# Feed-forward blocks of 256 and 290 token columns instead of 272 and 272

## The chip, the cores and the metric

The kernel runs on one core of one Trainium2 chip. The metric is device time of the program in microseconds (us), as the median of several runs. Beside the timed runs there is one execution recorded by the hardware profiler; all rows quoted below come from it.

The engines carry the profile's names: PE is the matmul engine (TensorE), PEld its weight loads, DVE the vector engine, ACT the scalar engine, POOL GpSimd, SP the engine that issues most transfers.

## The reference, cut to what matters

One decoder layer on 544 tokens: 512 of a prompt and 32 that are being decoded (8 sequences of 4). The layer is feed-forward block, mixer (a Mamba-2 group beside a sparse-attention group), feed-forward block, with a post-normalisation after each.

```python
def swiglu(x, w_gate, w_up, w_down):
    return (jax.nn.silu(x @ w_gate) * (x @ w_up)) @ w_down
...
h = layer_norm(ALPHA * x + 0.5 * swiglu(x, ffn1_w_gate, ffn1_w_up, ffn1_w_down), ln1_g, ln1_b)
mixed, state = mix_fn(h, lw, *mix_args)
h = layer_norm(ALPHA * h + mixed, ln2_g, ln2_b)
h = layer_norm(ALPHA * h + 0.5 * swiglu(h, ffn2_w_gate, ffn2_w_up, ffn2_w_down), ln3_g, ln3_b)
```

The model width is 1024, the feed-forward width 2816. All is computed to float32 accuracy.

## The kernel before

**Layout.** Tokens lie along the free dimension, channels on the 128 partitions. The 544 tokens stand as two halves of `HT` = 272 columns: `HP` = 256 prompt tokens and `HS` = 16 decoded ones each. The activations of a stage are eight tiles `XH[d]` and eight `XL[d]` (d = 0 to 7, the width in pieces of 128), each of two halves of 274 columns; columns 272 and 273 of half 0 hold, after a normalisation, its gain and bias, so that one matmul also yields the two sums per output channel that `fold` needs. Columns 272 and 273 of half 1 are never used.

**Matmuls.** Float32 accuracy is had by splitting each operand into a high part, rounded to the fast format float32r, and the rest: `XH` + `XL` for activations, `w_hi` + `w_lo` for weights. `gemm` (L256 to L265) makes three matmuls for each piece of 128 of the contraction: `w_hi` with the high part (L263), `w_hi` with the low part (L264), `w_lo` with the high part (L265). Each is preceded by a weight load of 128 columns. So one `gemm` over the model width is 8 x 3 = 24 matmuls into one PSUM tile.

**Feed-forward (`ffn`, L367).** Called twice. First 22 x 2 weight tiles (gate and up): for each weight tile one `gemm` per half h = 0, 1, then, on ACT and DVE, the Silu, the product and the split into `hH[:, f, h]` and `hL[:, f, h]`. In the second feed-forward block half 0 is multiplied with 274 columns. Then the eight output tiles of the down projection: 22 pieces x 3 matmuls for each half, in three weight tiles; `residual` adds the input on DVE, `Norm.tile` updates sums of the normalisation. For the last output tile (d = 7) half 0 is finished before half 1 begins, so that its tail can start.

**Order.** The program is written as loops, and a scheduler that simulates times places each instruction on its engine's queue; an engine runs its queue strictly in that order. Weights come by SP's queue through two raw buffers; ACT makes `w_hi` (L170), DVE or POOL `w_lo` (L171), three buffers each. The input x comes in four transfers (half 0 in two pieces of four tiles, then half 1), and ACT (L191) and DVE (L192) split each tile as it comes. The gate and up products use six PSUM tiles in turn.

Of the kernel before, what the change touches and what calls it, by code (L numbers as in the profile page):

```python
# [33 lines left out]

HP, HS = 256, 16
HT = HP + HS
D, KD = 1024, 8
DFF, KF = 2816, 22
ALPHA = 2.0 ** 0.25
# [136 lines left out]
def step_kernel(ctx, tc, I, O, stop=99):  # L176
    nc = tc.nc
    MUL, ADD, SUB, MAX = OP.mult, OP.add, OP.subtract, OP.max
# [4 lines left out]
    def f32(t):  # L183
        return t.bitcast(F32)
# [17 lines left out]
    eps1 = keep.tile([128, 1], F32, name="eps1")  # L202
    eps4 = keep.tile([128, 1], F32, name="eps4")
    XH, XL = [None] * KD, [None] * KD

    def new_x(d):
# [29 lines left out]
    with tc.tile_pool(name="xload", bufs=1) as xp:  # L236

        nc.vector.memset(eps1, LN_EPS)
        nc.scalar.activation(eps4, eps1, AF.Silu)
        W.load()  # L240
        for d in range(KD):
            new_x(d)
        for h in range(2):
            for a in range(2):
                xr = xp.tile([128, 4, HT], F32, name=f"xr{h}{a}")
                nc.sync.dma_start(xr, I["x"][h, :, 4 * a:4 * a + 4])
                if h == 0 and a == 1:
                    W.load()
                for d in range(4 * a, 4 * a + 4):
                    split(XH[d][:, h, :HT], XL[d][:, h, :HT], xr[:, d % 4])  # L250
        nc.gpsimd.dma_start(par, I["par"])
        cst(ident, "ident", nc.gpsimd)
        nc.vector.memset(ones, 1.0)
        nc.vector.memset(eps4, 4.0 * LN_EPS)

    def gemm(ps, wt, rhs, nk, k0=0, start=True, stop=True, m=128):  # L256

        hi, lo = wt
        rh, rl = rhs
# [18 lines left out]
    class Norm:  # L278
# [48 lines left out]

        def stats(self, pool, psum, halves=(0, 1), tag="st"):
            if 0 in halves:
                self.rstd = keep.tile([128, 2, HT], F32, name=f"rstd{self.n}", tag="rstd")  # L330
                self.nmr = keep.tile([128, 2, HT], F32, name=f"nmr{self.n}", tag="nmr")
# [18 lines left out]
        def fold(self, ps, h, cw, out, pool):  # L350

            m = cw.shape[0]
            if h == 0:
                nc.vector.tensor_copy(cw, ps[:m, HT:HT + 2])
            t = pool.tile([128, HT], F32, name="fold_t", bufs=2)
            nc.vector.tensor_tensor(t[:m], ps[:m, :HT], self.rstd[:m, h], op=MUL)
            nc.vector.scalar_tensor_tensor(out, self.nmr[:m, h], cw[:, 0:1], t[:m], op0=MUL, op1=ADD)

        def value(self, d, out, pool, mul):

# [6 lines left out]
    def ffn(pre, post, last):  # L367

        with tc.tile_pool(name="ffn", bufs=1) as fp, tc.tile_pool(name="ffn_ps", bufs=1, space=PS) as pp:
            hH = fp.tile([128, KF, 2, HT], F32R, name="hH")  # L370
            hL = fp.tile([128, KF, 2, HT], F32R, name="hL")
            with tc.tile_pool(name="ffn_g", bufs=1) as gp:
                for f in range(KF):
                    sg = {}
                    for which in range(2):
                        wt = W.get()
                        cw = gp.tile([128, 2], F32, name="cw", bufs=4)
                        for h in range(2):
                            ps = pp.tile([128, 512], F32, name="mm", bufs=6)
                            rh, rl, n = xcols(h, pre is not None)  # L380
                            gemm(ps[:, :n], wt, (rh, rl), KD)
                            if f == 0 and which == 0 and h == 0 and pre is not None:
                                pre.stats(gp, pp)
                            if pre is None:
                                src = ps[:, :HT]
                            else:
                                src = gp.tile([128, HT], F32, name="fold_o", bufs=2)
                                pre.fold(ps, h, cw, src, gp)
                            if which == 0:
                                sg[h] = gp.tile([128, HT], F32, name="sg", bufs=3)  # L390
                                if pre is None:
                                    nc.scalar.activation(sg[h], src, AF.Silu)
                                else:
                                    nc.scalar.activation(sg[h], src, AF.Silu, bias=cw[:, 1:2])
                            else:
                                hf = gp.tile([128, HT], F32, name="hf", bufs=2)
                                if pre is None:
                                    nc.vector.tensor_tensor(hf, src, sg[h], op=MUL)
                                else:
                                    nc.vector.scalar_tensor_tensor(hf, src, cw[:, 1:2], sg[h], op0=ADD, op1=MUL)  # L400
                                split(hH[:, f, h], hL[:, f, h], hf)
            with tc.tile_pool(name="ffn_d", bufs=1) as dp:
                nrm = Norm(dp, *post, eps4, to_x=not last)

                tab = dp.tile([128, 1], F32, name="tab")
                nc.scalar.activation(tab, f32(hH)[:, KF - 1, 1, 0:1], AF.Sqrt, scale=0.0, bias=eps1)
                for d in range(KD):
                    t = dp.tile([128, 2, HT], F32, name="res", bufs=2)
                    if pre is None:
# [6 lines left out]
                    def down(i, h):  # L416
                        gemm(ps[h][:, :HT], wts[i], (lambda k: hH[:, k, h], lambda k: hL[:, k, h]),
                             min(8, KF - 8 * i), 8 * i, start=i == 0, stop=i == 2)

                    def residual(h):  # L420
                        nc.vector.scalar_tensor_tensor(t[:, h], t[:, h], 2.0 * ALPHA, ps[h][:, :HT],
                                                       op0=MUL, op1=ADD)

                    if d < KD - 1:
                        for i in range(3):
                            for h in range(2):
                                down(i, h)
                        for h in range(2):
                            residual(h)
                        if d == 0:  # L430
                            nrm.mean0(t, dp, pp)
                        nrm.tile(d, t, dp)
                    else:
                        for h in range(2):
                            for i in range(3):
                                down(i, h)
                            residual(h)
# [1058 lines left out]
```

## Time and profile before

| what | value |
|---|---|
| runs | 1319.51, 1320.40, 1321.38 us; median 1320.4 |
| profiled execution | 1316.73 us, of which the span from first to last instruction is 1315.0 |
| mean granted clock of PE | 0.975 of full speed |
| PE busy | 1250.2 us (95%) |
| DVE, ACT, POOL busy | 778.3, 479.1, 355.0 us |
| gate and up of the first feed-forward block | about 6 to 276.5 us |
| its down projection | 276.5 to 410 us |
| mixer | 411 to 886 us |
| gate and up of the second block | 886 to 1158 us |
| its down projection and the end | 1158 to 1315 us |

A busy time of PE counts the time in which any matmul is on its way; since matmuls overlap (each lasts some 0.29 us, and the next starts well before it ends), the time that one costs in a row of many is the distance from its start to the next start. This text calls it the pitch.

### The profile page before, as it was taken

The page shows a single profiled execution, that of the slowest core. Times are in us where ns is not written, and L with a number is a line of the kernel's source. Part 1 is how long each engine was busy: PE and PEld are TensorE (multiplying, and loading weights), DVE is VectorE, ACT ScalarE, POOL GpSimd, SP SyncE. Part 2 cuts the span into 40 slices and gives each one's busy share as a digit, 9 for nine tenths or more (in the row PEclk, how much of TensorE's full clock was granted, in tenths as well). Part 3 has the DMA queues.
Part 4 walks back from the last instruction along what each step waited for, and adds up shares of the span by engine and source line. Part 5 has one row for each costly group of instructions (what it writes and reads, how often), then busy time and mean ns, then how long its engine had stood idle before and what let it go on. Part 6 is the DMA issues. An engine that isn't in the chain of part 4 may idle for free.

```text
span 1315.0 us, 24300 instructions
## 1 busy us (share of the span) xinstructions
PE 1250.2 (95%) x9768; PEld 1178.3 (90%) x9768; DVE 778.3 (59%) x1510; ACT 479.1 (36%) x900; POOL 355.0 (27%) x289
## 2 busy tenths in 40 slices
PE   8999999999999888999999999779999999999994
PEld 7999999999999788888887676779999999999993
DVE  4333333334336888766798685997666666644446
ACT  4322223232224445454554332434333333342213
POOL 0000000001333653453555542770000000035543
PEclk9999999999999997999999998989999999999997
DMA  5222232222324324532232651222222232323211
GB/s 204 81 89 88 82 96 81 90 80 89 89 89 146 128 75 147 143 128 85 38 98 39 200 207 63 65 64 81 81 91 87 81 96 81 90 80 89 89 57 68
DMA packets 63888, 126.74 MB, mean 96 GB/s; under 512 B 16168, under 2 KB 35312, under 8 KB 63776
## 3 DMA queue, kind: packets, MB, share of 16 engines
q1 hardware_dynamic: 61040, 116.52, 29.3%
q0 software_dynamic: 1584, 4.48, 1.0%
q10 hardware_dynamic: 1152, 4.19, 0.8%
q8 instruction: 77, 1.26, 0.4%
q14 instruction: 35, 0.29, 0.1%
HBM read 114.80 MB, written 9.36 MB: 94 GB/s over the span
## 4 chain that ended last, share of the span: by engine, by line
PE 52%; DVE 7%; issue 1%; ACT 1%; DMA 1%; POOL 1%; ACTq 0%; POOLq 0%; DVEq 0%
PE mm L265 12%; PE mm L264 12%; PE mm L263 12%; PE pv L915 3%; PE pj L263 2%; PE pj L264 2%; PE pj L265 2%; PE tp L925 1%; PE sc L884 1%; PE sc L886 1%; DMA win<-in_vwin 1%; DVE XL L311 1%; DVE XL L326 1%; PE tp L1266 1%; PE sg L975 0%
## 5 line engine op out<-in xcount | busy, mean ns | idle before, releaser
L263 PE MATMUL mm<-XH,w_hi 128*128 128x272 f32 (+1 forms) x1408 | 409.1, 291 | 11.8 <-ACT XH L191 6.3
L265 PE MATMUL mm<-XH,w_lo 128*128 128x272 f32 (+1 forms) x1408 | 409.4, 291 | 0.0
L264 PE MATMUL mm<-XL,w_hi 128*128 128x272 f32 (+1 forms) x1408 | 408.4, 290 | 0.3 <-DVE XL L192 0.3
L171 DVE TENSOR_TENSOR w_lo<-w_raw,w_hi 128x1024 fp32r<-128x1024 f32 x149 | 183.6, 1232 | 205.1 <-ACT w_hi L170 203.4
L170 ACT ACTIVATE w_hi<-w_raw 128x1024 fp32r<-128x1024 f32 (+1 forms) x173 | 179.2, 1036 | 284.5 <-PE mm L264 231.9
L263 PEld LDWEIGHTS mm<-XH,w_hi 128*128 128x128 f32 x1408 | 268.1, 191 | 12.4 <-ACT XH L191 6.5
L264 PEld LDWEIGHTS mm<-XL,w_hi 128*128 128x128 f32 x1408 | 268.6, 191 | 0.7 <-DVE XL L192 0.6
L265 PEld LDWEIGHTS mm<-XH,w_lo 128*128 128x128 f32 x1408 | 267.4, 190 | 0.1
L265 PE MATMUL mm<-hH,w_lo 128*128 128x272 f32 x704 | 203.9, 290 | 0.0
L264 PE MATMUL mm<-hL,w_hi 128*128 128x272 f32 x704 | 203.4, 289 | 0.0
L263 PE MATMUL mm<-hH,w_hi 128*128 128x272 f32 x704 | 203.0, 288 | 0.0
L272 POOL TENSOR_TENSOR res<-XH,XL 128x544 f32<-128x544 f32 x24 | 35.0, 1468 | 588.9 <-DVE hL L192 550.0
L264 PEld LDWEIGHTS mm<-hL,w_hi 128*128 128x128 f32 x704 | 132.6, 188 | 0.2
L263 PEld LDWEIGHTS mm<-hH,w_hi 128*128 128x128 f32 x704 | 132.5, 188 | 0.1
L265 PEld LDWEIGHTS mm<-hH,w_lo 128*128 128x128 f32 x704 | 132.3, 188 | 0.2
L263 PE MATMUL pj<-XH,w_hi 128*128 128x272 f32 (+3 forms) x336 | 99.9, 297 | 7.0 <-DVE pj_u L640 5.8
L265 PE MATMUL pj<-XH,w_lo 128*128 128x272 f32 (+3 forms) x336 | 98.8, 294 | 0.0
L264 PE MATMUL pj<-XL,w_hi 128*128 128x272 f32 (+3 forms) x336 | 98.2, 292 | 0.0
L191 ACT ACTIVATE hH<-hf 128x272 fp32r<-128x272 f32 x88 | 37.5, 426 | 144.7 <-DVE hf L400 98.0
L263 PEld LDWEIGHTS pj<-XH,w_hi 128*128 128x128 f32 (+1 forms) x336 | 62.4, 186 | 11.2 <-issue 7.3
L321 POOL TENSOR_TENSOR accS<-res,accS 128x544 f32<-128x544 f32 x18 | 35.7, 1982 | 121.5 <-DVE res L307 121.5
L171 POOL TENSOR_TENSOR w_lo<-w_raw,w_hi 128x1024 fp32r<-128x1024 f32 (+1 forms) x24 | 56.8, 2365 | 38.4 <-ACT w_hi L170 38.4
(423 smaller groups left out, 2146.8 us busy)
## 6 DMA issues: line engine op xcount, KB each, us to landing
w_raw<-in_wg SPq DMA_DIRECT2D x44, 512.0 KB, 3.5
w_raw<-in_wu SPq DMA_DIRECT2D x44, 512.0 KB, 3.5
w_raw<-in_wd SPq DMA_DIRECT2D x32, 512.0 KB, 3.5
w_raw<-in_win SPq DMA_DIRECT2D x20, 512.0 KB, 3.6
pg<-in_cmp SPq DMA_DIRECT2D x64, 128.0 KB, 2.4
w_raw<-in_wd SPq DMA_DIRECT2D x16, 384.0 KB, 3.1
w_raw<-in_w SPq DMA_DIRECT2D x8, 512.0 KB, 3.7
pg<-in_kslc SPq DMA_DIRECT2D x64, 64.0 KB, 1.9
```

What stands on the lines that cost most here:

```text
L170: nc.scalar.activation(hi[:, :nk, :m], raw[:, :nk, :m], AF.Copy)
L171: (eng or nc.vector).tensor_tensor(lo[:, :nk, :m], raw[:, :nk, :m], hi.bitcast(F32)[:, :nk, :m], op=OP.subtract)
L191: nc.scalar.activation(hi, src, AF.Copy)
L263: nc.tensor.matmul(ps, hi[:, k, :m], rh(k0 + k), start=b, stop=False)
L264: nc.tensor.matmul(ps, hi[:, k, :m], rl(k0 + k), start=False, stop=False)
L265: nc.tensor.matmul(ps, lo[:, k, :m], rh(k0 + k), start=False, stop=e)
L272: nc.gpsimd.tensor_tensor(out, a, b, op=ADD)
L311: nc.vector.scalar_tensor_tensor(XL[d][:, h, :HT], s[:, h], self.g[:, d:d + 1], f32(XH[d])[:, h, :HT], op0=MUL, op1=SUB)
L321: eng.tensor_tensor(acc[:, h], v[:, h], acc[:, h], op=ADD)
L326: nc.vector.tensor_tensor(XL[d][o], col[:, d:d + 1], f32(XH[d])[o], op=SUB)
L884: nc.tensor.matmul(s, q, S.K[:, br, h // 4, 0, :w], start=True, stop=False)
L915: nc.tensor.matmul(pv[hh * 64:hh * 64 + 64, hp % 2], v, t[:, hh], start=start, stop=stop)
```

## The change

The 2 x 274 columns of an activation tile are now taken as one flat row of 548, of which columns 0 to 545 are multiplied, in two blocks: columns 0 to 255 (the first 256 prompt tokens) and columns 256 to 545 (16 decoded tokens, the two extra columns, the whole second half): 256 and 290 columns. `hH` and `hL` get rows of 548 columns. For each weight tile of gate and up the block of 290 stands first. `fold`, the Silu, the product and the split work on blocks. In the down projection of d = 0 to 6 the blocks replace the halves, and `residual` is three DVE instructions instead of two; d = 7 keeps halves of 272. New small memsets on POOL clear the two extra columns where nothing else writes them; two constants share one tile.

```diff
+WT = HT + 2
+BLK = (slice(0, HP), slice(HP, HT + WT))
...
+                    if h == 0:
+                        for t in (XH[d], XL[d]):
+                            nc.gpsimd.memset(f32(t)[:, 0, HT:], 0.0)
                     split(XH[d][:, h, :HT], XL[d][:, h, :HT], xr[:, d % 4])
...
+    def flat(t):
+        return t.rearrange("p a b -> p (a b)")
+
+    def xblk(c):
+        return (lambda k: flat(XH[k])[:, c]), (lambda k: flat(XL[k])[:, c])
...
-            hH = fp.tile([128, KF, 2, HT], F32R, name="hH")
-            hL = fp.tile([128, KF, 2, HT], F32R, name="hL")
+            hH = fp.tile([128, KF, 2 * WT], F32R, name="hH")
+            hL = fp.tile([128, KF, 2 * WT], F32R, name="hL")
...
-                        for h in range(2):
-                            ps = pp.tile([128, 512], F32, name="mm", bufs=6)
-                            rh, rl, n = xcols(h, pre is not None)
-                            gemm(ps[:, :n], wt, (rh, rl), KD)
-                            if f == 0 and which == 0 and h == 0 and pre is not None:
+                        for i in (1, 0):
+                            c = BLK[i]
+                            n = c.stop - c.start
+                            ps = pp.tile([128, 512], F32, name="mm", bufs=6)[:, :n]
+                            gemm(ps, wt, xblk(c), KD)
+                            if f == 0 and which == 0 and i == 1 and pre is not None:
                                 pre.stats(gp, pp)
...
                         for i in range(3):
-                            for h in range(2):
-                                down(i, h)
-                        for h in range(2):
-                            residual(h)
+                            for p, c in zip(ps, BLK):
+                                down(i, p, c)
+                        residual(t[:, 0, :HP], ps[0][:, :HP])
+                        residual(t[:, 0, HP:], ps[1][:, :HS])
+                        residual(t[:, 1], ps[1][:, HS + 2:HS + 2 + HT])
```

PE's queue at the start of the program, before: the last matmuls of the first `gemm` (PSUM tile mm_154, half 0 of all eight tiles), and then the first matmul that reads half 1 (into mm_181).

```order
L265 MATMUL mm_154<-XH6_85,w_lo_150 128x272
L263 MATMUL mm_154<-XH7_87,w_hi_149 128x272
L264 MATMUL mm_154<-XL7_88,w_hi_149 128x272
L265 MATMUL mm_154<-XH7_87,w_lo_150 128x272
L263 MATMUL mm_181<-XH0_73,w_hi_149 128x272
```

PE's queue at the same place now: mm_169 is the block of 290, mm_196 the block of 256 of the first weight tile.

```order
L270 MATMUL mm_169<-XH0_72,w_hi_164 128x290
L270 MATMUL mm_196<-XH0_72,w_hi_164 128x256
L271 MATMUL mm_196<-XL0_73,w_hi_164 128x256
L272 MATMUL mm_196<-XH0_72,w_lo_165 128x256
L270 MATMUL mm_196<-XH1_74,w_hi_164 128x256
```

A matmul that reads both halves of tile 0 is now PE's very first instruction; the 24 matmuls that read half 0 alone stood ahead of any such before.

DVE's queue early in the mixer, before, where `cp_lo` belongs to the compression of the prompt's keys and `QS` to the queries:

```order
L666 TENSOR_TENSOR pj_f_5363<-pj_f_5363,pj_sw_5364 128x544
L751 TENSOR_TENSOR cp_lo_5289<-cp_kc_5285,KcH_4332 64x32
L733 COPY cp_t_5445<-mm_5384 128x2
L751 TENSOR_TENSOR cp_lo_5295<-cp_kc_5285,KcH_4332 64x32
L734 TENSOR_TENSOR peb_4306<-cp_t_5445,mm_5384 128x1
L702 SCALAR_TENSOR_TENSOR QS_4320<-pj_f_5363,QS_4320 64x2x256 x2
```

And now:

```order
L687 TENSOR_TENSOR pj_f_5387<-pj_f_5387,pj_sw_5388 128x544
L723 SCALAR_TENSOR_TENSOR QS_4342<-pj_f_5387,QS_4342 64x2x256
L754 COPY cp_t_5469<-mm_5408 128x2
L723 SCALAR_TENSOR_TENSOR QS_4342<-pj_f_5387,QS_4342 64x2x256
L755 TENSOR_TENSOR peb_4328<-cp_t_5469,mm_5408 128x1
L175 TENSOR_TENSOR w_lo_5866<-w_raw_5863,w_hi_5865 128x1024
```

The scheduler moved the queries ahead of the compressed keys; further down that queue, for some 150 rows, attention steps and compression steps of the mixer are interleaved in another order, though no line of the mixer was edited.

## Rows read from the trace of the kernel before

**Rows 1.** Busy time of each engine in three stretches.
```profile
core 0: us, PE busy (x) PEld busy (x) DVE busy (x) ACT busy (x) POOL busy (x), PEclk, DMA share, GB/s
40.00:400.00 360.00, 360.00 (x2846) 359.84 (x2845) 129.51 (x187) 103.83 (x174) 33.48 (x20) 1.00 0.28 87
900.00:1157.00 257.00, 257.00 (x2027) 257.00 (x2026) 171.46 (x346) 89.40 (x133) 0.00 (x0) 1.00 0.28 88
500.00:520.00 20.00, 15.24 (x75) 14.95 (x76) 17.88 (x31) 10.55 (x24) 4.53 (x3) 0.57 0.62 174
```

**Rows 2.** Line L264: count, duration, first and last start; gate/up, then down, first block.
```profile
L264 PE MATMUL mm<-XL,w_hi x675: 286/289/294, 19.9 to 276.3; 128*128 128x272 f32 x169
...
L264 PE MATMUL mm<-hL,w_hi x284: 283/288/297, 297.9 to 404.8; 128*128 128x272 f32 x142
```

**Rows 3.** Timeline of PE, second block: start, duration; first matmuls of three successive gemms.
```profile
1017.98 0.28 PE L263 MATMUL mm<-XH,w_hi 128*128 128x274 f32 x1
...
1021.02 0.29 PE L263 MATMUL mm<-XH,w_hi 128*128 128x272 f32 x1
...
1024.07 0.28 PE L263 MATMUL mm<-XH,w_hi 128*128 128x274 f32 x1
```

**Rows 4.** Timeline of PE in the mixer: first and last of three runs of 256-column matmuls.
```profile
518.95 0.28 PE L263 MATMUL mm<-cs_H,w_hi 128*128 128x256 f32 x1
...
522.58 0.28 PE L265 MATMUL mm<-cs_H,w_lo 128*128 128x256 f32 x1
...
532.96 0.29 PE L264 MATMUL mm<-cs_L,w_hi 128*128 128x256 f32 x1
...
534.16 0.28 PE L265 MATMUL mm<-cs_H,w_lo 128*128 128x256 f32 x1
...
606.97 0.28 PE L263 MATMUL mm<-cs_H,w_hi 128*128 128x256 f32 x1
...
610.16 0.28 PE L263 MATMUL mm<-cs_H,w_hi 128*128 128x256 f32 x1
```

**Rows 5.** Timeline of PE in the mixer: one matmul of 512 columns and the next.
```profile
666.59 0.39 PE L884 MATMUL sc<-K,QS 128*128 128x512 f32 x1
666.82 0.23 PE L885 MATMUL sc<-mk_d,idb 128*128 128x128 bf16 x1
```

**Rows 6.** Timeline of PE in the mixer: matmuls of 66 columns at a lower clock, first and last of 27.
```profile
505.50 0.40 PE L263 MATMUL mm<-cH,w_hi 128*128 128x66 f32 x1
...
511.05 0.40 PE L265 MATMUL mm<-cH,w_lo 128*128 128x66 f32 x1
```

**Rows 7.** Timeline of PE at the start of the program.
```profile
6.25 0.59 PE L263 MATMUL mm<-XH,w_hi 128*128 128x272 f32 x1 [6.25 <-ACT XH L191]
...
8.21 0.43 PE L265 MATMUL mm<-XH,w_lo 128*128 128x272 f32 x1
...
10.02 0.41 PE L264 MATMUL mm<-XL,w_hi 128*128 128x272 f32 x1
10.24 0.31 PE L265 MATMUL mm<-XH,w_lo 128*128 128x272 f32 x1
10.39 0.29 PE L263 MATMUL mm<-XH,w_hi 128*128 128x272 f32 x1
...
11.40 0.29 PE L265 MATMUL mm<-XH,w_lo 128*128 128x272 f32 x1
11.69 0.52 PE L263 MATMUL mm<-XH,w_hi 128*128 128x272 f32 x2
```

**Rows 8.** Timeline of ACT: the splits of half 1, tiles 0 to 3, then 4 to 7.
```profile
11.21 1.40 ACT L191 ACTIVATE XH<-xr 128x272 fp32r<-128x272 f32 x4 [0.54 <-DMA xr<-in_x]
...
12.78 1.39 ACT L191 ACTIVATE XH<-xr 128x272 fp32r<-128x272 f32 x4
```

**Rows 9.** Start of the second block: PE, then DVE, then the busy time of a stretch.
```profile
885.74 0.57 PE L263 MATMUL mm<-XH,w_hi 128*128 128x274 f32 x1 [5.59 <-DVE res L607]
...
890.67 0.41 PE L263 MATMUL mm<-XH,w_hi 128*128 128x272 f32 x1
...
889.97 0.49 DVE L311 SCALAR_TENSOR_TENSOR XL<-res,par,XH 128x272 fp32r<-128x272 f32 x1
...
885.70:890.60 4.90, 4.86 (x21) 4.89 (x22) 4.76 (x9) 1.69 (x4) 0.74 (x1) 0.50 0.42 149
```

More of the change, by code (lines that the diff above doesn't have):

```diff
@@ L201, in step_kernel @@
     ones = keep.tile([128, 128], F32, name="ones")
-    eps1 = keep.tile([128, 1], F32, name="eps1")
-    eps4 = keep.tile([128, 1], F32, name="eps4")
+    eps = keep.tile([128, 2], F32, name="eps")
+    eps1, eps4 = eps[:, 0:1], eps[:, 1:2]
     XH, XL = [None] * KD, [None] * KD
@@ L329, in stats @@
             if 0 in halves:
-                self.rstd = keep.tile([128, 2, HT], F32, name=f"rstd{self.n}", tag="rstd")
-                self.nmr = keep.tile([128, 2, HT], F32, name=f"nmr{self.n}", tag="nmr")
+                self.rstd_w = keep.tile([128, 2, WT], F32, name=f"rstd{self.n}", tag="rstd")
+                self.nmr_w = keep.tile([128, 2, WT], F32, name=f"nmr{self.n}", tag="nmr")
+                self.rstd, self.nmr = (t[:, :, :HT] for t in (self.rstd_w, self.nmr_w))
+                if self.to_x:
+                    for t in (self.rstd_w, self.nmr_w):
+                        nc.gpsimd.memset(t[:, 0, HT:], 0.0)
             for h in halves:
@@ L348, in stats, with fold @@
                 nc.vector.scalar_tensor_tensor(self.nmr[:, h], mq[:, 0], -1.0, self.rstd[:, h], op0=MUL, op1=MUL)
[L350 to L357, printed above, removed]
+        def fold(self, ps, c, cw, out, pool):
+            n = c.stop - c.start
+            if c.start:
+                nc.vector.tensor_copy(cw, ps[:, HS:HS + 2])
+            t = pool.tile([128, BLK[1].stop - HP], F32, name="fold_t", bufs=2)
+            nc.vector.tensor_tensor(t[:, :n], ps, flat(self.rstd_w)[:, c], op=MUL)
+            nc.vector.scalar_tensor_tensor(out, flat(self.nmr_w)[:, c], cw[:, 0:1], t[:, :n], op0=MUL, op1=ADD)
         def value(self, d, out, pool, mul):
@@ L369, in ffn @@
         with tc.tile_pool(name="ffn", bufs=1) as fp, tc.tile_pool(name="ffn_ps", bufs=1, space=PS) as pp:
-            hH = fp.tile([128, KF, 2, HT], F32R, name="hH")
-            hL = fp.tile([128, KF, 2, HT], F32R, name="hL")
+            hH = fp.tile([128, KF, 2 * WT], F32R, name="hH")
+            hL = fp.tile([128, KF, 2 * WT], F32R, name="hL")
             with tc.tile_pool(name="ffn_g", bufs=1) as gp:
+                wide = BLK[1].stop - HP
                 for f in range(KF):
@@ L377, in ffn @@
                         cw = gp.tile([128, 2], F32, name="cw", bufs=4)
-                        for h in range(2):
-                            ps = pp.tile([128, 512], F32, name="mm", bufs=6)
-                            rh, rl, n = xcols(h, pre is not None)
-                            gemm(ps[:, :n], wt, (rh, rl), KD)
-                            if f == 0 and which == 0 and h == 0 and pre is not None:
+                        for i in (1, 0):
+                            c = BLK[i]
+                            n = c.stop - c.start
+                            ps = pp.tile([128, 512], F32, name="mm", bufs=6)[:, :n]
+                            gemm(ps, wt, xblk(c), KD)
+                            if f == 0 and which == 0 and i == 1 and pre is not None:
@@ L383, in ffn @@
                                 pre.stats(gp, pp)
                             if pre is None:
-                                src = ps[:, :HT]
+                                src = ps
                             else:
-                                src = gp.tile([128, HT], F32, name="fold_o", bufs=2)
-                                pre.fold(ps, h, cw, src, gp)
+                                src = gp.tile([128, wide], F32, name="fold_o", bufs=2)[:, :n]
+                                pre.fold(ps, c, cw, src, gp)
@@ L389, in ffn @@
                             if which == 0:
-                                sg[h] = gp.tile([128, HT], F32, name="sg", bufs=3)
+                                sg[i] = gp.tile([128, wide], F32, name="sg", bufs=3)[:, :n]
                                 if pre is None:
-                                    nc.scalar.activation(sg[h], src, AF.Silu)
+                                    nc.scalar.activation(sg[i], src, AF.Silu)
                                 else:
-                                    nc.scalar.activation(sg[h], src, AF.Silu, bias=cw[:, 1:2])
+                                    nc.scalar.activation(sg[i], src, AF.Silu, bias=cw[:, 1:2])
@@ L395, in ffn @@
                             else:
-                                hf = gp.tile([128, HT], F32, name="hf", bufs=2)
+                                hf = gp.tile([128, wide], F32, name="hf", bufs=2)[:, :n]
                                 if pre is None:
-                                    nc.vector.tensor_tensor(hf, src, sg[h], op=MUL)
+                                    nc.vector.tensor_tensor(hf, src, sg[i], op=MUL)
                                 else:
-                                    nc.vector.scalar_tensor_tensor(hf, src, cw[:, 1:2], sg[h], op0=ADD, op1=MUL)
@@ L401, in ffn @@
-                                split(hH[:, f, h], hL[:, f, h], hf)
+                                    nc.vector.scalar_tensor_tensor(hf, src, cw[:, 1:2], sg[i], op0=ADD, op1=MUL)
+                                split(hH[:, f, c], hL[:, f, c], hf)
             with tc.tile_pool(name="ffn_d", bufs=1) as dp:
@@ L405, in ffn @@
                 tab = dp.tile([128, 1], F32, name="tab")
-                nc.scalar.activation(tab, f32(hH)[:, KF - 1, 1, 0:1], AF.Sqrt, scale=0.0, bias=eps1)
+                nc.scalar.activation(tab, f32(hH)[:, KF - 1, 0:1], AF.Sqrt, scale=0.0, bias=eps1)
                 for d in range(KD):
@@ L414, in ffn, with down, residual @@
                     wts = [W.get() for _ in range(3)]
-                    def down(i, h):
-                        gemm(ps[h][:, :HT], wts[i], (lambda k: hH[:, k, h], lambda k: hL[:, k, h]),
+                    def down(i, p, c):
+                        gemm(p[:, :c.stop - c.start], wts[i], (lambda k: hH[:, k, c], lambda k: hL[:, k, c]),
                              min(8, KF - 8 * i), 8 * i, start=i == 0, stop=i == 2)
-                    def residual(h):
-                        nc.vector.scalar_tensor_tensor(t[:, h], t[:, h], 2.0 * ALPHA, ps[h][:, :HT],
-                                                       op0=MUL, op1=ADD)
+                    def residual(o, p):
+                        nc.vector.scalar_tensor_tensor(o, o, 2.0 * ALPHA, p, op0=MUL, op1=ADD)
                     if d < KD - 1:
                         for i in range(3):
-                            for h in range(2):
-                                down(i, h)
-                        for h in range(2):
-                            residual(h)
+                            for p, c in zip(ps, BLK):
[3 more added lines that the diff above has]
+                        residual(t[:, 1], ps[1][:, HS + 2:HS + 2 + HT])
                         if d == 0:
@@ L435, in ffn @@
                             for i in range(3):
-                                down(i, h)
-                            residual(h)
+                                down(i, ps[h], slice(h * WT, h * WT + HT))
+                            residual(t[:, h], ps[h][:, :HT])
                             nrm.tile(d, t, dp, slice(h, h + 1))
```

## The prediction

> **What bounds the kernel now.** I read the busy time of the engines by stretch first [rows 1]. In the gate and up stage of either feed-forward block PE is busy all of the stretch (360.00 of 360 us, 257.00 of 257) at a granted clock of 1.00, while DVE is busy 36% and 67% and ACT less. So PE never waits there: the two blocks go as fast as PE can follow one matmul with the next, and what one costs is the pitch. The third stretch, in the mixer, is the contrast: PE busy 15.24 of 20 us, clock 0.57.
>
> The pitches come from first and last starts. Line L264 is every third matmul [rows 2]: gate and up of the first block (276.3 - 19.9) / 674 / 3 = 126.8 ns; down (404.8 - 297.9) / 283 / 3 = 125.9. In the second block 24 matmuls of 274 columns begin at 1017.98, 24 of 272 at 1021.02, the next 274 at 1024.07 [rows 3]: 6.09 / 24 = 253.8 ns for a pair (one of each), 126.9 for one.
>
> At 2.4 GHz 272 columns stream in 113.3 ns and 274 in 114.2. So each matmul costs 12.6 to 13.5 ns beyond its columns. I call this the extra. Its size for 256 and for 290 columns decides the case, since the sum of columns hardly changes.
>
> **The change part by part.**
>
> *Counts.* Gate and up: 44 weight tiles x 24 = 1056 pairs in each block. Down: 7 output tiles x 66 = 462 pairs in each, 924 in both. Nothing is removed: 3036 pairs of 272/274 become 3036 pairs of 256 and 290, the columns of a pair from 544 to 546 (first gate and up, both downs) or 546 as before (second gate and up).
>
> *The block of 256.* The stream is 106.7 ns. The mixer has runs of such matmuls, with a weight load each, through the same `gemm` [rows 4]: (522.58 - 518.95) / 32 = 113.4 ns, (534.16 - 532.96) / 10 = 120.0, (610.16 - 606.97) / 27 = 118.1. The extra is thus 6.7 to 13.3, in three runs of one shape. The floor is near: 66 columns at the lower clock have a pitch of (511.05 - 505.50) / 26 = 213 ns [rows 6], which is 256 clocks of 1.2 GHz and far more than 66; so the weight load sets it, and if it takes as many clocks at 2.4 GHz, it is 106.7 ns, just the stream of 256. In that position the extra may well change from run to run. I take 116.7, the middle of the ends (113.4 + 120.0) / 2.
>
> *The block of 290.* The stream is 120.8 ns, and no row has this width. Neighbours: 272 with an extra of 13, and 512 [rows 5]: 0.23 us, a stream of 213.3, hence an extra of 16.7. From below the smallest extra, 6.7, gives 127.5; from above 16.7 gives 137.5. I take 133.8, an extra of 13, by the nearest row: 290 stands 18 columns from 272 and 222 from 512.
>
> *The sum of the stream.* A pair then costs 116.7 + 133.8 = 250.5 ns. First gate and up: 250.5 - 253.6 = -3.1 ns x 1056 = -3.3 us. Second: 250.5 - 253.8 = -3.3 x 1056 = -3.4 us. Down: 250.5 - 251.8 = -1.3 x 924 = -1.2 us. Together -7.9 us.
>
> *The head.* PE's first matmul now reads both halves of tile 0. Before, PE starts at 6.25 us, when half 0 of tile 0 is split, and at 11.69 first reads half 1 [rows 7], whose splits on ACT begin at 11.21 for the first four tiles and at 12.78 for the others, 0.35 us apart [rows 8]. In between it does 24 matmuls. These now come behind 11.69: 24 x 126.8 ns = 3.04 us. And the engine has its slow beginning later. Starting from idle at 6.25, its matmuls have a pitch of (10.02 - 8.21) / 8 = 226 ns until about 10.24, which is 272 columns at 1.2 GHz, and then speed up; at 885.74, after 5.59 us of idle, the clock is 0.50 until 890.6 [rows 9]. So 4.0 to 4.9 us at the lower level, of which each loses 1 - 126.8 / 226 = 0.44 us. Before, this fell into the time in which half 1 was awaited anyway; now it lies on the path: 1.8 to 2.2 us, and I take 1.8 since the stretch at the very start is the nearer row. The head costs +4.8 us (4.8 to 5.2). The later splits don't add: three matmuls of one tile take three low pitches, 0.7 us, and tiles come each 0.35. All of this reaches the end, for nothing in the 260 us behind it is idle and could absorb it.
>
> *The second block's start.* There PE waits 5.59 us for DVE's residual sum of the last output tile, and its first `gemm` now needs half 1 too. The last split of half 1 on DVE ends at 889.97 + 0.49 = 890.46. The first matmul that needs it is the 23rd; 22 of 290 columns at 1.2 GHz (242 ns) from 885.74 end at 891.1. So it costs nothing, by 0.6 us; if that cover fails, some tenths.
>
> *Work beside.* The third residual instruction in each output tile, the wider `fold`, the memsets and the products on blocks lie on DVE, ACT and POOL, and are hidden as long as DVE stays under PE's pace: 171.46 us of 257 is its fullest stretch [rows 1], and some per cent more leaves it far from full. An uncovered residual instruction would cost a half microsecond for each of 14 tiles at worst; I take 0, since PSUM tiles are used in turn.
>
> *The mixer.* Its order changes though its lines don't. In 20 us of it PE has 4.76 us of idle time [rows 1], so a displaced step can cost or bring a few microseconds. I know no sign for it and take 0, bounds -4.8 and +4.8.
>
> *Total.* -7.9 + 4.8 = -3.1 us. The sum is made on the profiled execution: 1316.7 - 3.1 = 1313.6. That run stands 3.7 us below the median of the three runs; the difference carries over: 1320.4 - 3.1 = **1317.3 us**.
>
> **The rivals.**
>
> *A, as worked out:* -3.1 us, 1317.3. Its own range follows from the bounds that are near: 256 at 115.5 to 118 and the head at 5.2: 1313 to 1321. With 290 at 133.8 the 256 block breaks even when the pairs gain 4.8 us / 3036 = 1.6 ns on average, that is, at 117.8.
>
> *B, the narrow block runs as in its best stretch,* 113.4 ns all along. For: the 32 gaps there are the longest run. Against: the two others. A pair is 247.2 ns: -6.4 x 1.056 - 6.6 x 1.056 - 4.6 x 0.924 = -17.9 us; with the head -13.1: 1307.3.
>
> *C, on the other side: the extra stays what it is today for both widths.* Then nothing is won by the split. The two more columns of a pair cost 0.83 ns, x 1056 = 0.9 us in the first gate and up, 0 in the second, x 924 = 0.8 us in the downs, and the head's 4.8 us stay: +6.5, 1326.9. For: 272, 274 and one 256 run have 12.6 to 13.5. Against: 6.7 in another 256 run. It decides as soon as the 256 block has a pitch of 118 or more. The Trainium skill ("TensorE: Matmul & The Clock Gate", section "Back-to-back issue gap") gives, for a matmul by itself, the columns over 2.4 GHz and some 2.5 ns: a constant beside the columns, so by it too the split would bring nothing in the stream. The trace has 126.9 where this gives 115.8 to 116.7, and an extra that differs between runs of one width, so the rule is not borne out in size; its form has the chance of C.
>
> *D, the wide block pays what the 512-wide row pays,* 137.5. A pair is 254.2: +0.6 x 1.056 + 0.4 x 1.056 + 2.4 x 0.924 = +3.3 us; with the head +8.1: 1328.5. For it speaks only that far row.
>
> *E, the mixer's order decides,* by over 3 us in either sense: 1312 to 1322 around A.
>
> **How the numbers follow.** A 0.42, B 0.17, C 0.25, D 0.11, E 0.05. What a measurement of this kernel tells from no change is about 0.2%, 2.6 us. A's centre is just over that: of its 0.42 I give 0.26 to faster, 0.14 to the same and 0.02 to slower. B is faster. Of C 0.22 is slower and 0.03 the same, of D 0.09 and 0.02, of E 0.02 faster, 0.01 the same, 0.02 slower. So faster 0.45, the same 0.20, slower 0.35. The range takes in B and, at the other end, C and part of D: 1306 to 1328.
>
> **What would show it.** In the profile after: PE's first matmul at about 11.7 us instead of 6.25, and its slow pitch until some 4 us later; in the middle of a gate and up stage, 24 matmuls of 256 columns take 2.80 us from start to start and 24 of 290 take 3.21 if A is right; 2.72 for the narrow ones in B, 2.87 in C, 3.30 for the wide ones in D. The second block begins with a wait of about 5.6 us and no second one within 6 us. The mixer lasts 475 us as before (411 to 886). The prediction is wrong above all if the pitch of 256 columns is not near 117, then if 290 columns have another extra than 13, and if the mixer moves by more than 3 us.

## The result, and the profile after

The changed kernel takes 1330.66 us (median of 4 runs, 1329.74 to 1331.68), the kernel before in the same comparison 1319.95 (1318.42 to 1321.38). The ratio is 1.0082, 95% interval 1.0064 to 1.0099: slower by 10.7 us, 0.8%. A gain of 3.1 us was forecast.

The profiled execution took 1329.74 us, its span is 1328.0, 13.0 above that of before. That is more than the 10.7 of the medians, since the profiled run of before was a quick one. Cut at the first and last matmuls of the stages, the span divides as follows (us, from the starts in the two traces):

| stretch | before | after | difference |
|---|---|---|---|
| to PE's first matmul | 6.25 | 11.24 | +4.99 |
| first feed-forward block, to its last matmul | 403.89 | 403.75 | -0.14 |
| mixer, to the second block's first matmul | 475.60 | 485.31 | +9.71 |
| second feed-forward block, to its last matmul | 407.83 | 406.68 | -1.15 |
| rest | 21.43 | 21.02 | -0.41 |

So the blocks that were changed take what they took; the loss stands at the start and in the mixer, no line of which was edited. The rows of PE's timeline at the borders of the mixer, after:

```profile
414.99 0.29 PE L272 MATMUL mm<-hH,w_lo 128*128 128x272 f32 x1
...
900.30 0.58 PE L270 MATMUL mm<-XH,w_hi 128*128 128x290 f32 x1 [5.15 <-DVE res L628]
```

The second row is the wait for the residual sum that [rows 9] show before, 5.59 us there.

The busy time by stretch, after, in the two gate and up stages:

```profile
40.00:400.00 360.00, 360.00 (x2846) 359.84 (x2845) 127.88 (x195) 103.81 (x174) 29.74 (x19) 1.00 0.28 87
900.00:1157.00 257.00, 256.70 (x2008) 256.41 (x2009) 173.60 (x349) 87.18 (x132) 1.01 (x1) 0.99 0.28 87
```

Beside [rows 1]: PE is as full as before (256.70 because the second stage only begins at 900.30), DVE hardly changed. What a pair costs stands in PE's timeline, first matmuls of successive gemms (24 each), in the second gate and up stage and then in the first down projection, after:

```profile
1019.14 0.30 PE L270 MATMUL mm<-XH,w_hi 128*128 128x290 f32 x1
...
1022.39 0.28 PE L270 MATMUL mm<-XH,w_hi 128*128 128x256 f32 x1
...
1025.22 0.30 PE L270 MATMUL mm<-XH,w_hi 128*128 128x290 f32 x1
```

```profile
331.81 0.28 PE L270 MATMUL mm<-hH,w_hi 128*128 128x256 f32 x1
...
334.65 0.30 PE L270 MATMUL mm<-hH,w_hi 128*128 128x290 f32 x1
...
337.86 0.28 PE L270 MATMUL mm<-hH,w_hi 128*128 128x256 f32 x1
```

Gate and up: 290 columns 3.25 / 24 = 135.4 ns, 256 columns 2.83 / 24 = 117.9; together 253.3 where [rows 3] give 253.8. Down: 118.3 + 133.8 = 252.1 in this one pair, 118.0 + 133.7 = 251.7 in the mean of the stage's 14 gemms of 24 matmuls for each width, where it was 251.8. So over the whole kernel the narrow blocks save about as much as the wide ones cost more: the difference is about 1 us.

The start of the program on PE's timeline, after:

```profile
11.24 0.79 PE L270 MATMUL mm<-XH,w_hi 128*128 128x290 f32 x2 [11.24 <-ACT XH L195]
11.83 0.42 PE L271 MATMUL mm<-XL,w_hi 128*128 128x256 f32 x1
...
15.68 0.44 PE L271 MATMUL mm<-XL,w_hi 128*128 128x290 f32 x1
15.91 0.35 PE L272 MATMUL mm<-XH,w_lo 128*128 128x290 f32 x1
16.11 0.30 PE L270 MATMUL mm<-XH,w_hi 128*128 128x290 f32 x1
```

PE begins 5.0 us later than in [rows 7] and is slow for 4.7 us from there, as it was for 4.0 us before. At the end of the first feed-forward block it is 414.99 - 410.14 = 4.85 us late.

In the mixer PE comes to one place that it did not wait at before: the transpose of `ge_a` in the second compression step. The timelines of PE, ACT, DVE and POOL there, after:

```profile
573.37 0.64 PE L1232 MATMUL tp<-par,ge_a 128*128 128x64 f32 x4
...
574.93 0.36 PE L907 MATMUL sc<-K,QS 128*128 128x256 f32 x1
577.45 0.70 PE L1230 MATMUL tp<-ge_a,par 128*64 128x128 f32 x4 [2.15 <-DVE ge_a L502]
...
574.22 0.41 ACT L498 ACTIVATE ge_a<-cs_x 128x256 f32<-128x256 f32 x1
...
574.08 1.11 DVE L917 TENSOR_TENSOR at_m<-at_m,G 128x1 f32<-128x1 f32 x2
575.12 0.28 DVE L499 TENSOR_SCALAR ge_a<-ge_a 128x256 f32<-128x256 f32 x1
...
576.97 0.42 DVE L502 SCALAR_TENSOR_TENSOR ge_a<-ge_a,cs_x 128x256 f32<-128x256 f32 x1 [0.48 <-ACT ge_a L501]
...
572.25 2.86 POOL L1216 TENSOR_TENSOR cs_L<-pg,cs_H 128x1024 fp32r<-128x1024 f32 x1 [0.88 <-ACT cs_H L1215]
```

and before:

```profile
564.98 0.66 PE L1211 MATMUL tp<-par,ge_a 128*128 128x64 f32 x4
...
568.24 0.37 PE L886 MATMUL sc<-K,QS 128*128 128x256 f32 x1
568.44 0.28 PE L264 MATMUL mm<-cs_L,w_hi 128*128 128x256 f32 x1
...
570.26 0.28 PE L265 MATMUL mm<-cs_H,w_lo 128*128 128x256 f32 x1
570.47 0.44 PE L1209 MATMUL tp<-ge_a,par 128*64 128x128 f32 x4
...
565.85 0.41 ACT L477 ACTIVATE ge_a<-cs_x 128x256 f32<-128x256 f32 x1
...
568.16 0.42 DVE L481 SCALAR_TENSOR_TENSOR ge_a<-ge_a,cs_x 128x256 f32<-128x256 f32 x1
```

Before, 17 matmuls of `cs` stood between the scores and the transpose, and DVE had finished `ge_a` at 568.58, 1.9 us ahead of need. After, the scheduler has put these 17 matmuls elsewhere, and most of the scores with the compressed keys, 1.7 us of work (565.93 to 567.63 before), ahead of L1232. That matters because `ge_a` has a single buffer (`bufs=1`): its next chain of steps on ACT and DVE begins only when PE has read the old content, in L1232 (L1211 before). From there to the transpose PE had 5.5 us of other work before (564.98 to 570.47) and has 1.9 us now (573.37 to 575.29, the end of the scores); the chain is ready 3.6 us after that reading begins before, and 4.0 us after it now.

The 0.4 us more lie on DVE, which begins its three steps of `ge_a` late: the step ahead of them, two tiny products of one column, ends at 575.19 instead of within 0.3 us, together with POOL's split of `cs_L` (572.25 + 2.86 = 575.11). PE stands still for 2.15 us and is then slow, as the busy time of a stretch at this place shows (after, then before):

```profile
575.80:582.60 6.80, 5.15 (x25) 4.62 (x26) 4.81 (x15) 3.32 (x10) 1.54 (x3) 0.50 0.00 0
```

```profile
568.50:577.00 8.50, 8.50 (x74) 7.81 (x73) 6.51 (x15) 4.62 (x11) 2.66 (x2) 1.00 0.53 217
```

The granted clock is 0.50, the 1.2 GHz level, for 6.8 us; before it was 1.00. Half of 6.8 us is the most that the lower level can lose, so the stall and the slow stretch together are worth at most 2.15 + 3.4 = 5.6 us (an estimate).

### The profile page after: what moved, and what is told of

Same layout as the page of the kernel before. It is cut to its first block, busy times and chain, and to the rows that moved or that the text cites. A ratio compares the mean times of both kernels' runs of the same rounds, so it can differ in the third digit from the quotient of the medians.

```text
span 1328.0 us, 24353 instructions
## 1 busy us (share of the span) xinstructions
PE 1257.3 (95%) x9768; PEld 1183.7 (89%) x9768; DVE 780.3 (59%) x1524; ACT 477.2 (36%) x898; POOL 355.9 (27%) x309
## 4 chain that ended last, share of the span: by engine, by line
PE 50%; DVE 8%; ACT 2%; issue 2%; DMA 1%; POOL 1%; POOLq 0%; SPq 0%; ACTq 0%; DVEq 0%
PE mm L270 11%; PE mm L272 11%; PE mm L271 11%; PE pv L936 3%; PE pj L270 2%; PE pj L271 2%; PE pj L272 2%; PE tp L946 1%; PE sc L905 1%; PE sc L907 1%; DVE XL L324 1%; DVE w_lo L175 1%; PE tp L1287 1%; DVE XL L339 1%; PE sg L996 0%
## 5 line engine op out<-in xcount | busy, mean ns | idle before, releaser
L270 PE MATMUL mm<-XH,w_hi 128*128 128x290 f32 (+1 forms) x1408 | 409.0, 291 | 16.4 <-ACT XH L195 11.2
L271 PE MATMUL mm<-XL,w_hi 128*128 128x256 f32 (+1 forms) x1408 | 409.2, 291 | 0.0
L272 PE MATMUL mm<-XH,w_lo 128*128 128x256 f32 (+1 forms) x1408 | 408.8, 290 | 0.0
L270 PEld LDWEIGHTS mm<-XH,w_hi 128*128 128x128 f32 x1408 | 267.8, 190 | 16.7 <-issue 16.5
L272 PE MATMUL mm<-hH,w_lo 128*128 128x256 f32 (+2 forms) x704 | 204.0, 290 | 0.0
L270 PE MATMUL mm<-hH,w_hi 128*128 128x256 f32 (+2 forms) x704 | 203.5, 289 | 0.0
L271 PE MATMUL mm<-hL,w_hi 128*128 128x256 f32 (+2 forms) x704 | 203.4, 289 | 0.0
L195 ACT ACTIVATE hH<-hf 128x290 fp32r<-128x290 f32 x88 | 37.5, 428 | 157.2 <-DVE hf L421 102.5
```

## The experiments

Ten kernels were run. Theory O: the order which the scheduler gave the mixer costs. Theory T: the mixer is slow because it begins later. Theory B: the new blocks make it slow. "Old order" and "new order" are those of the mixer in the kernel before and in the changed kernel.

**narrow_first.** The only edit that matters to the chip is the first weight tile:

```diff
-for i in (1, 0):
+for i in ((0, 1) if f + which == 0 else (1, 0)) if pre is None else (1, 0):
```

> The changed kernel, with the narrow block ahead of the wide one in the very first weight tile alone, so that PE begins with half 0 as it did before; the scheduler then gives the mixer the order that it had before. Theory O (the longer mixer belongs to the order that the scheduler gave it): first matmul at about 6.3 us, mixer 475.6 us instead of 485.3, the feed-forward stages as in the changed kernel; the sum of those stage differences is -0.5 + 0.4 - 1.5 + 0.4 - 0.4 = -1.6, so about 1.6 us under the kernel before. Theory T (the mixer is longer because it begins some 4.5 us later): the same, since it begins at the old time. Theory B (the wide blocks themselves, by what they do to PE's clock, lengthen the mixer): mixer near 485, 8 us over the kernel before.

Measured: 1321.08 us against 1320.38, ratio 1.0002 (0.9992 to 1.0011). PE begins at 6.35; the mixer lasts 481.05 us in the profile. All 3036 pairs are 256 and 290, and the loss is gone: B falls, and the new blocks are worth nothing in either direction that these runs could tell (about 1.5 us).

**half1_first.** The opposite: the changed kernel's code with the halves of before as its blocks, half 1 first in the first weight tile.

```diff
+GU = (slice(0, HT), slice(WT, WT + HT)) if pre is None else (slice(0, WT), slice(WT, WT + HT))
+DN = (slice(0, HT), slice(WT, WT + HT)) if pre is None else (slice(0, HT), slice(WT, WT + HT))
...
-for i in (1, 0):
+for i in ((1, 0) if f + which == 0 else (0, 1)) if pre is None else (0, 1):
```

> The blocks of before (272 and 272, or 274 and 272) in all stages, but half 1 ahead of half 0 in the very first weight tile; nothing of 256 and 290. The scheduler gives the mixer the order that the changed kernel has. Theories O and T: first matmul at about 11.3 to 11.7 us (+5), mixer 485 (+9.7), the whole 14 to 15 us over the kernel before, the full loss without the new blocks. Theory B: mixer 475.6, the whole 5 us over.

Measured: 1330.2 us against 1320.38, ratio 1.0065 (1.0046 to 1.0084). PE begins at 11.05, the mixer lasts 484.5, and the stall is there with 2.15 us. The whole loss comes without the new blocks. It is 9.8 us by the medians, not the 14 to 15 that the profiled executions gave.

**x_interleaved.** Loads of x in another order:

```diff
-for h in range(2):
-    for a in range(2):
+for h, a in ((0, 0), (1, 0), (0, 1), (1, 1)):
```

> The changed kernel with its four loads of x in another order: both halves of tiles 0 to 3, then both halves of tiles 4 to 7. The mixer keeps the order of the changed kernel. Theory O: PE begins 2 to 4 us earlier than in the changed kernel, the mixer still lasts 485 us, so 2 to 4 us under the changed kernel and 9 to 11 us over the kernel before by its profile. Theory T: the mixer begins nearly at the old time and lasts about 476, so about the kernel before.

Measured: 1329.46 us against 1320.38, ratio 1.0066 (1.0049 to 1.0083): 9.1 us over the kernel before. PE begins at 8.51, the mixer at 412.2, and it lasts 485.8 us. It begins 1.4 us behind that of narrow_first and is 4.7 us longer, so the lateness is a poor explanation; but the clock differs from one execution to the next, and the pairs below were made to decide it.

**narrow_late.**

```diff
+dly = xp.tile([128, 512], F32, name="dly")
+nc.gpsimd.memset(dly, 0.0)
+for _ in range(9):
+    nc.scalar.activation(dly, dly, AF.Copy)
```

> As narrow_first, with nine copies of a 128x512 tile on ACT ahead of the splits of x, which do nothing but make PE begin some 5 us later; the mixer has the order that it had before. Theory O: everything is later by the delay at the start, about 5 us, and the mixer lasts 475.6 us; some 3.5 us over the kernel before. Theory T: the mixer is 485 us as in the changed kernel, some 13 us over the kernel before.

Measured: 1319.32 us against 1320.38, ratio 0.9997 (0.9986 to 1.0009). It says nothing of lateness: the scheduler put the splits of x between the copies, and PE began at 6.17. It is a second run of the old order with the new blocks: mixer 476.3 us.

**early_new_order and late_old_order** cross the two: the head of one kernel with the mixer's order of the other. The scheduler's order depends on simulated times, and a few matmuls more in the first block move it:

```diff
 gemm(ps, wt, xblk(c), KD)       # f == 4, gate, narrow block only, ahead of it:
+for q in range(5):              # 4 in late_old_order
+    nc.tensor.matmul(ps, wt[0][:, q % 8, :], xblk(c)[0](q % 8), start=q == 0, stop=q == 4)
```

> As narrow_first, with five more matmuls of 256 columns in one gate tile of the first feed-forward block (0.6 us, their result is overwritten); with them the scheduler gives the mixer exactly the order that the changed kernel has on PE, POOL and SP, though PE begins at 6.3 us. Theory O (the order costs): mixer 484 to 486 us, the whole 5 to 10 us over narrow_first. Theory T (the later start costs): mixer 476 to 481, the whole 0.6 us over narrow_first.

> The changed kernel with four more matmuls of 256 columns in the same gate tile (0.5 us, overwritten); with them the scheduler gives the mixer the order of before but for nine places in PE's queue of some 2470, while PE still begins at about 11.2 us. Theory O: mixer 476 to 481, so that of the loss only the head (5 us) and the 0.5 us are left: 5 to 6 us over the kernel before. Theory T: mixer 485, 10 to 11 us over the kernel before.

Measured, by the medians, each kernel against the kernel before in its own comparison (1320.38 for narrow_first, 1319.62 for the next two, 1319.95 for the changed kernel):

| head | mixer's order | kernel | mixer in the profile | us over the kernel before (ratio) |
|---|---|---|---|---|
| early | old | narrow_first | 481.05 | +0.7 (0.9992 to 1.0011) |
| early | new | early_new_order | 482.7 | +5.2, 4.6 without the added 0.6 (1.0013 to 1.0046) |
| late | old | late_old_order | 480.0 | +5.1, 4.6 without the added 0.5 (1.0023 to 1.0048) |
| late | new | the changed kernel | 485.3 | +10.7 (1.0064 to 1.0099) |

By the medians head and order each cost about 4.6 us. The ratios of the runs put them somewhat lower: 1.0036 for late_old_order, which is 4.2 us for the head, and 1.0029 for early_new_order, which is 3.2 us for the order, with an interval of 1.1 to 5.5 us. So the order costs something clear of noise, but its size is known only to some 2 us. Together the two make the loss of 10.7 us within the intervals; 1 to 3 us of it may belong to neither alone. Theory T falls as the main cause: with the late head (PE begins at 11.77 there) and the old order the whole is only 5.1 us over, which the head uses up. Theory O holds, at half the size or less that the profiled executions had shown.

In one profile the mixer of a given order differs by up to 5.5 us from the next one (475.6 to 481.05 in the old order), since stretches at the lower clock come and go; so a mixer's time alone tells little, and the place of the stall more. PE's timeline there, early_new_order and then late_old_order:

```profile
571.30 0.36 PE L915 MATMUL sc<-K,QS 128*128 128x256 f32 x1
573.82 0.69 PE L1238 MATMUL tp<-ge_a,par 128*64 128x128 f32 x4 [2.15 <-DVE ge_a L510]
```

```profile
577.47 0.28 PE L273 MATMUL mm<-cs_H,w_lo 128*128 128x256 f32 x1
577.67 0.44 PE L1238 MATMUL tp<-ge_a,par 128*64 128x128 f32 x4
```

All four kernels in the new order wait 2.15 or 2.16 us here and are at 0.50 for 6.8 us behind it, and so does widths_b (below), which got the new order too; none in the old order waits here. From the first to the last matmul of `cs`, the stretch in which the orders differ, the new order takes 101.4 to 102.3 us (five kernels), the old 96.3 to 100.5 (before, narrow_first, narrow_late, late_old_order, second_only). The whole mixer takes 481.6 to 485.8 us in those five and 475.6 to 481.05 in these.

**third_order**, with six added matmuls instead of five.

> As early_new_order with six more matmuls instead of five (0.7 us); the scheduler then gives the mixer a third order, in 34 places another than that of before and in 32 another than that of the changed kernel. In the changed kernel's order PE comes to the transpose of ge_a (second compression step, some 162 us into the mixer) with none of the 17 matmuls of cs ahead of it that stand there in the order of before, and waits 2.16 us; in this third order 2 stand there. Theory S (that stall, and the low clock behind it, make the order cost what it does): a stall of some 1.9 us at this place, 101 us or more from the first to the last cs matmul instead of 96.4 to 100.5, and about 5 us over the kernel before, as early_new_order. Theory R (any other order costs or brings something, from many places): no stall needed, the time anywhere within 5 us of the kernel before.

Measured: 1327.32 us against 1319.0, ratio 1.0055 (1.0033 to 1.0078): 8.3 us slower, with an early head. The place was right and the size was not: the stall is 5.33 us, and the stretch of `cs` takes 105.1. PE, ACT, DVE and POOL there, and the busy time behind it:

```profile
571.85 0.28 PE L273 MATMUL mm<-cs_H,w_lo 128*128 128x256 f32 x1
577.46 0.69 PE L1238 MATMUL tp<-ge_a,par 128*64 128x128 f32 x4 [5.33 <-DVE ge_a L510]
...
571.17 0.28 ACT L1242 ACTIVATE vcS<-tp 128x128 f32<-128x128 f32 x1 [3.25 <-DMA win<-in_kwin]
572.53 2.00 ACT L1223 ACTIVATE cs_H<-pg 128x1024 fp32r<-128x1024 f32 x2 [0.78 <-PE mm L273]
...
572.33 0.42 DVE L508 TENSOR_TENSOR ge_a<-ge_a,cs_x 128x256 f32<-128x256 f32 x1
...
574.87 2.44 DVE L510 SCALAR_TENSOR_TENSOR ge_a<-ge_a,cs_x 128x256 f32<-128x256 f32 x1
...
574.62 2.42 POOL L1224 TENSOR_TENSOR cs_L<-pg,cs_H 128x1024 fp32r<-128x1024 f32 x1 [5.68 <-ACT cs_H L1223]
...
575.30:582.10 6.80, 4.64 (x23) 4.23 (x24) 5.59 (x13) 2.87 (x9) 2.36 (x3) 0.50 0.00 0
```

DVE's last step of `ge_a`, 0.42 us elsewhere, takes 2.44: it begins 0.25 us after POOL's split of `cs_L` and ends 0.27 us after it. So the stall is longest where that step and the split meet. That hold is 2.0 us; the rest of the delay is ACT's, which waits for a transfer until 571.17 before it begins the chain, and runs both splits of `cs_H` (572.53 to 574.53) between two steps of it. Against early_new_order the stall is 3.2 us longer and the whole, by the medians, 3.1 us slower, so theory S is supported in place and mechanism. Its 1.9 us were wrong because they counted only the matmuls that were left as cover, and not how long the chain takes. The Trainium skill ("SBUF — State Buffer", section "Who interferes with whom") says that a DVE instruction with two SBUF inputs contends with a GpSimd instruction that reads SBUF, and that the port pair which they share is an exclusive lock. Both steps that were held have two such inputs, and the trace agrees: 2.44 us beside the split, 0.42 without it.

**second_only.** The first call of `ffn` keeps halves of 272:

```diff
+GU = (slice(0, HT), slice(WT, WT + HT)) if pre is None else BLK
+DN = (slice(0, HT), slice(WT, WT + HT)) if pre is None else BLK
```

> The first feed-forward block as in the kernel before, the second as in the changed kernel, so the change reaches only what lies behind the mixer, and the mixer keeps its order on PE and POOL. Theory C (256 and 290 columns cost together what 272 and 274 cost): no change within 0.2%. Theory A of the prediction (256 columns at 116.7 ns, 290 at 133.8): 4 us faster, of which 3.4 in the gate and up stage.

Measured: 1320.0 us against 1319.0, ratio 0.9997 (0.998 to 1.0013). The interval shuts out a gain of 4 us, so the sum is theory C's.

**widths_a and widths_b.** The cut at other columns in each of the four stages; `GU` is the cut of gate and up, `DN` that of the down projection, here those of widths_a (in widths_b 200 and 240, then 34 and 128):

```diff
+GU = (slice(0, 34), slice(34, HT + WT)) if pre is None else (slice(0, 128), slice(128, HT + WT))
+DN = (slice(0, 200), slice(200, HT + WT)) if pre is None else (slice(0, 240), slice(240, HT + WT))
```

> As narrow_first, with other places of the cut in each stage: 34 and 512 columns in the first gate and up, 200 and 346 in its down, 128 and 418 in the second gate and up, 240 and 306 in its down. Read from it is the pitch of each width. Theory C (a constant extra of 13 ns beside the columns, and a floor set by the weight load): 512 at 226, 418 at 187, 346 at 157, 306 at 140.5, and all narrow ones near one floor of 111 to 118. Theory P (each column costs 0.466 ns, 12% over the stream, so the split is neutral by itself): 512 at 239, 418 at 195, 346 at 161, 306 at 143. If the floor is at 118, then 256 was already set by its weight load.

> As widths_a with the cuts exchanged between gate and up and down: 200 and 346, 34 and 512 (down), 240 and 306, 128 and 418 (down). It tells whether a width costs the same in the two kinds of stage: in the changed kernel 290 columns cost 135.4 ns in gate and up and 133.8 in down. Both theories expect the numbers of widths_a within 2 ns.

PE's timeline, first matmuls of successive gemms of 24, in gate and up: first widths_a (34 and 512, then 128 and 418), then widths_b (200 and 346, then 306 and 240).

```profile
196.19 0.18 PE L271 MATMUL mm<-XH,w_hi 128*128 128x34 f32 x1
...
198.79 0.48 PE L271 MATMUL mm<-XH,w_hi 128*128 128x512 f32 x1
...
204.50 0.18 PE L271 MATMUL mm<-XH,w_hi 128*128 128x34 f32 x1
...
1107.95 0.22 PE L271 MATMUL mm<-XH,w_hi 128*128 128x128 f32 x1
1110.57 0.40 PE L271 MATMUL mm<-XH,w_hi 128*128 128x418 f32 x1
1115.22 0.22 PE L271 MATMUL mm<-XH,w_hi 128*128 128x128 f32 x1
```

```profile
202.65 0.26 PE L271 MATMUL mm<-XH,w_hi 128*128 128x200 f32 x1
205.31 0.34 PE L271 MATMUL mm<-XH,w_hi 128*128 128x346 f32 x1
209.15 0.26 PE L271 MATMUL mm<-XH,w_hi 128*128 128x200 f32 x1
...
1100.22 0.31 PE L271 MATMUL mm<-XH,w_hi 128*128 128x306 f32 x1
1103.61 0.28 PE L271 MATMUL mm<-XH,w_hi 128*128 128x240 f32 x1
1106.30 0.31 PE L271 MATMUL mm<-XH,w_hi 128*128 128x306 f32 x1
```

Each distance over 24 gives the pitch:

| cut | narrow, ns | wide, ns | pair, ns |
|---|---|---|---|
| 34 + 512 | 108.3 | 237.9 | 346.2 |
| 128 + 418 | 109.2 | 193.8 | 303.0 |
| 200 + 346 | 110.8 | 160.0 | 270.8 |
| 240 + 306 | 112.1 | 141.3 | 253.4 |
| 256 + 290 (the changed kernel) | 117.9 | 135.4 | 253.3 |
| 274 + 272 (before) | | | 253.8 |

Theory P comes within 2 ns of every wide block, theory C lies 0.8 to 12 under. From 272 to 512 columns the pitch rises by (237.9 - 126.8) / 240 = 0.46 ns a column. Below some 240 columns it stays at 108 to 112, which no narrower block gets under; 256 columns lie above it. So the three cuts that keep both blocks at 240 or more cost the same, and the narrower ones lose. Between the two kinds of stage a width differs by up to 1.6 ns (290: 135.4 and 133.8); in the mixer 256 columns had 113.4 to 120.0 [rows 4], so the width is not all that counts, and what else does is open. The whole kernels took 1531.8 and 1422.0 us (one run each).

## Why the prediction was wrong

**The head** was right: +4.8 us forecast, 4.85 at the end of the first block, and 4.2 to 4.6 by late_old_order. PE begins at 11.24 and not at 11.69, and most of its slow matmuls are narrow ones, for the scheduler let the narrow gemm run behind the first wide matmuls.

**The stream** is the first step that failed. It was to bring 7.9 us, as 116.7 ns for 256 columns and 133.8 for 290. In gate and up the two are 117.9 and 135.4, so a pair saves 0.3 to 0.5 ns instead of 3.1 to 3.3; in the downs the mean of 251.7 saves 0.1 instead of 1.3. That is -0.3 - 0.5 - 0.1 = -0.9 us. (The prediction's product for the second gate and up, -3.3 x 1056, is -3.5 us and not -3.4; that changes nothing.) The mistake was to take the extra of 290 columns for that of 272 (13) while that of 256 was taken from the mixer's short runs at 10. The extra grows with the columns: 117.9 - 106.7 = 11.2, 13.5, 14.6 and, at 512, 24.6. In gate and up the two widths were missed by 1.2 and 1.6 ns, in the downs 256 alone by 1.3; 3036 pairs made that nearly the whole gain. The 16.7 at 512 columns [rows 5] was one row followed by a matmul of another kind, and too low.

**The mixer** is the second step that failed: "I know no sign for it and take 0". Its order costs 3.2 to 4.6 us by early_new_order, inside the bound of 4.8 that was set for it; in the profiled executions it is 9.7, where other stretches at the lower clock add to it (the mean granted clock of the mixer is 0.96 before and 0.93 after). The rows that showed the moved queue entries stood in the part on the change, and the chance of 0.05 for case E was too small for a stage that has such moved rows and PE's low clock behind each stall.

**The rest.** The work beside was hidden as forecast: DVE is busy 173.60 of 257 us. The second block begins with one wait and no second; its -1.15 us in the stage table are mostly a shorter slow beginning (0.50 for 4.9 us in [rows 9]; a mean of 0.67 over 4.8 us after) and no property of the change.

**The rivals.** C, at 1326.9, came nearest, and rightly in that the split brings nothing; it lacked E. Its reason, an extra that is the same for both widths, was wrong. So was here the form of the rule of the Trainium skill that stood beside it ("TensorE: Matmul & The Clock Gate", section "Back-to-back issue gap"), a constant beside the columns: the extra grew from 11.2 to 24.6 ns. The measured 1330.66 lies outside the range, which had no case with C and E together.

**What stays open.** In the part of the mixer behind the stretch of `cs`, where all the orders agree, the kernels take 272.6 to 278.5 us; why the changed kernel is among the long ones was not separated from the changing clock. The four kernels whose PE begins late (the changed one, half1_first, x_interleaved, late_old_order) are the four longest there, at 276.8 to 278.5 against 272.6 to 276.5 for the eight others, so a smaller part of theory T, of a few microseconds in the profiles, is not shut out; the medians of late_old_order leave little room for it. That the stall and the slow stretch behind it are all that the order costs was not shown: a kernel with the new order but without the stall was not made, since an edit that moves instructions can make the scheduler order the mixer anew, as the added matmuls did. No version that was run beats the kernel before clear of its interval.

## What to carry to other kernels

Where matmuls with a weight load each follow one another without gaps, measure the pitch by width in that stage before cutting columns otherwise: here it was flat up to some 240 columns and nearly proportional above, so the cuts tried above that were neutral, and the time was decided by what else they changed. When instructions are placed by a scheduler that works with simulated times, an edit at the start reorders stages far behind it; compare the orders, look for a chain whose cover (the other work that its reader has meanwhile) has gone, and price that as a term of its own. Of a block that reads data loaded in pieces, begin with what the first piece feeds.

## What the runs showed of the hardware

The clock fell in a stage in which PE was busy without a gap. In widths_a's gate and up of 34 and 512 columns it fell at about 190.0 us, 1.1 us after a run of 24 matmuls of 34 columns had ended; the busy time of the stretch behind that, and of the next, is:

```profile
190.00:193.40 3.40, 3.40 (x10) 2.63 (x9) 1.23 (x1) 0.21 (x2) 0.00 (x0) 0.50 0.28 53
193.50:200.00 6.50, 6.50 (x42) 5.77 (x41) 1.58 (x3) 1.72 (x3) 0.00 (x0) 1.00 0.13 52
```

This stage has a mean granted clock of 0.86 from 40 to 400 us, where the stages of 272 columns or of 256 and 290 have 1.00. And a DVE instruction can be held by POOL for some 2 us: the same one took 0.42 us alone and 2.44 us beside a POOL instruction of 2.42 us. This was so in the kernel before, too, where it cost PE no wait: a DVE product of one column, 0.16 us elsewhere, took 1.69 us from 561.76 and ended at 563.45, with POOL's split of `cs_L` (560.98 + 2.46 = 563.44).
